# Softmax sums divided after the value product, and wo's norms and last weights placed elsewhere

## The chip, the cores and the metric

The kernel runs on one core of a Trainium2 chip. Its engines are TensorE (PE in the profile, with its weight loads as PEld), VectorE (DVE), ScalarE (ACT), GpSimd (POOL) and SyncE (SP, which here only issues DMAs). Each engine works through its own list of instructions in order. The metric is the device time of one execution in microseconds; the number before the change is the median of three runs.

## The reference, cut to what matters

One decoder layer on 1024 tokens of width 1024, in float32. Two SwiGLU half-steps stand around a token mixer with two branches, and the change touches branch A's softmax and the norms behind the mixer's output projection:

```
# branch A, for each head: scores against the selected keys, softmax, values
p = jax.nn.softmax(s, axis=-1)
o = p @ values
# the mixer's end, and the start of the second SwiGLU
y = (sigmoid(g_a) * (o_a @ w_up_a) + sigmoid(g_b) * (o_b @ w_up_b)) @ w_o
x = x + gt2 * rms_norm(y, g_post_mix)
h = rms_norm(x, g_pre_ffn2) * (1 + sc3) + sh3
x = x + 0.5 * gt3 * rms_norm(swiglu(h, w_gate2, w_up2, w_down2), g_post_ffn2)
```

## The kernel before

**Order.** The program is written in one order and then laid out for each engine by a scheduler ahead of time, with modelled costs; on the chip every engine keeps the order that it was given, and semaphores make it wait. Float32 products are made from three matmuls (`mm3`, lines L104 to L106), on a high part and a low part of each operand. `split` (L76, L77) makes these parts: ScalarE casts, VectorE subtracts; `psplit` (L81, L82) subtracts on GpSimd instead.

**Branch A** (`branch_a`) has four head pairs p, two heads e, four token groups g and two token tiles t = 2g, 2g + 1 in each. `scores` makes the masked scores of one tile in a buffer `aP` (six of them, shared in a ring) and their maximum (L1058, VectorE), takes the exponential on ScalarE with the row sum into `st` (L1061), inverts the sum on VectorE (L1062) and multiplies the whole tile by it on GpSimd (L1063). `mix` transposes the tile on TensorE (L1081, `apt`), splits it, and after the second tile of a group multiplies with the values (L1091, `apv`) into one PSUM bank of 512 columns, of which 256 are used. That bank, tag `o`, exists once. ScalarE copies one half out (L1095), VectorE adds the other (L1097); then the bank is free. There are 32 such products. During the third head pair, `combine_b` joins branch B's groups, eight times: small VectorE operations of 4 or 12 columns on `cM`, `ce` and `br` (L951 to L960) and three GpSimd operations (L962 to L964).

**wo.** The output projection is done in four quarters: token half h (0, 1), column half c (0, 1). A quarter has 96 matmuls: four token tiles j, eight pieces k of the contraction, three each. Its weights are 16 tiles (a high and a low part for each k) from pool `W`, which has 13; the next weights, of the second SwiGLU, use the same 13. With 13, the last three of a quarter must wait for the first three, so all four token tiles are worked on side by side in four PSUM banks, and end together. `evac` (L365, L366) takes a bank out and collects the row's squares. After each half, per token tile: `residual` adds up the squares, takes a reciprocal root and adds onto the residual stream `xt` (L1160), a DMA writes it away, and `prenorm` squares it on ScalarE (L1165), takes a second root and scales (L1168). A root is `rsqrt`, eight instructions of one column each (L88, L89, then three pairs of L94 and L95), on VectorE for four of the sixteen and on GpSimd for the other twelve. `xt` of half 1 is read, 2 MB at once, into a buffer of tag `z`; that of half 0 has tag `gab`.

**After wo.** `first_half` transposes half 0 (L208), scales it (L214, L216) and splits it into V[0] and V[1]; `second_half` does so with half 1 and makes V[2] to V[6] from sums and differences (L232). `gate_up` multiplies V[i] with weights for blocks b; the program has it start with V[0] and V[1] for three blocks (144 matmuls) and then go on to V[2].

Of the kernel before, what the change touches and what calls it, by code (L numbers as in the profile page):

```python
# [10 lines left out]
F32 = mybir.dt.float32  # L11
F32R = mybir.dt.float32r
# [8 lines left out]
D = 1024  # L21
# [18 lines left out]
class Layer:  # L40
# [453 lines left out]
        nc.vector.tensor_tensor(out1, out1, t[0], op=ALU.subtract)  # L494
        nc.vector.tensor_tensor(out2, out2, t[1], op=ALU.add)

    def load_w(self, W, src, n, name, rows=1024, per=None, split=None, rawp=None):

        nc = self.nc
        per = per or 1024 // n  # L500
        his, los = [], []
        nk = rows // P
        for k0 in range(0, nk, per):
            m = min(per, nk - k0)
            r = (rawp or self.rawp).tile([P, m, n], F32, name=f"{name}r", tag="raw")
            nc.sync.dma_start(r, src[k0 * P:(k0 + m) * P, :].rearrange("(k p) f -> p k f", p=P))
            for j in range(m):
                hi = W.tile([P, n], F32R, name=f"{name}h", tag="w")
                lo = W.tile([P, n], F32R, name=f"{name}l", tag="w")
                (split or self.split)(hi, lo, r[:, j, :])  # L510
                his.append(hi)
                los.append(lo)
        return his, los
# [457 lines left out]
    def branch_a(self, aw, ap, late, G, mask, off):  # L971
# [73 lines left out]
        def scores(p, e, g, t):  # L1045

            K, Q, n = KE[p % 2][e], QQ[:, e], (t + 1) * P
            Pm = ap.tile([P, S], F32, name="aP", bufs=NAP)[:, :n]
            mx = late.tile([P, 2], F32, name="mx", bufs=4)
            st = late.tile([P, 2], F32, name="st", bufs=4)  # L1050
            nb = (n + 511) // 512
            for c in range(nb):
                m = min(512, n - 512 * c)
                b = self.bank("as", tag=next(banks))
                self.mm3(b[:, :m], Q[:, 0, t, :], Q[:, 1, t, :],
                         K[:, 0, 512 * c:512 * c + m], K[:, 1, 512 * c:512 * c + m], True, True)
                mk = self.tri[:, 256 - n:] if t < 2 else mask[:, off[t] + 512 * c:off[t] + 512 * c + m]
                nc.vector.tensor_tensor_reduce(Pm[:, 512 * c:512 * c + m], b[:, :m], mk, -scale,  # L1058
                                               mx[:, 0:1] if c else 3.0e38,
                                               op0=ALU.add, op1=ALU.min, accum_out=mx[:, c:c + 1])  # L1060
            nc.scalar.activation(Pm, Pm, AF.Exp, bias=mx[:, nb - 1:nb], scale=-1.0, accum_out=st[:, 1:2])  # L1061
            nc.vector.reciprocal(st[:, 1:2], st[:, 1:2])  # L1062
            nc.gpsimd.tensor_tensor(Pm, Pm, st[:, 1:2].to_broadcast([P, n]), op=ALU.mult)  # L1063
            state[p, e, t] = Pm

        def mix(p, e, g, t):

            nj = 2 * g + 2
            if t == 2 * g:
# [18 lines left out]
            for j in range(nj):  # L1088
                q0 = max(0, j - 2 * g) * P
                for l in range(2):  # L1090
                    nc.tensor.matmul(b[:, q0:256], VV[p][:, j, e, :], pt[j // 4][l][:, j % 4, q0:],  # L1091
                                     start=j == 0 and l == 0, stop=j == nj - 1 and l == 1)
            main, oth = slice(64 * e, 64 * e + 64), slice(64 - 64 * e, 128 - 64 * e)
            tmp = late.tile([P, 256], F32, name="otmp", bufs=2)
            nc.scalar.copy(tmp[main, :], b[oth, :256])  # L1095
            od = of[g // 2][main, (g % 2) * 256:(g % 2 + 1) * 256]
            nc.vector.tensor_add(od, b[main, :256], tmp[main, :])  # L1097
            if p == 2:
                self.combine_b(late, state["oB"], 4 * e + g)
            if e == 1 and g == 0:  # L1100
# [72 lines left out]
def layer_kernel(ctx, tc, aps, out):  # L1173
# [136 lines left out]
    with pool("w3", 13) as W, pool("r5", 3) as L.rawp, pool("o2") as op:  # L1310
# [5 lines left out]
        with pool("zp") as zp:  # L1316
# [6 lines left out]
            ss = sums()  # L1323
            for h in range(2):
                ys[h] = L.big.tile([P, 4, D], F32, name=f"wy{h}", tag="big")
                xt = zp.tile([P, 4, D], F32, name=f"xt{h}", **(dict(tag="z", bufs=3) if h else dict(tag="gab")))
                nc.sync.dma_start(xt, L.x1[4 * h * P:(4 * h + 4) * P, :].rearrange("(t p) d -> p t d", p=P))
                for c in range(2):
                    cl = slice(c * 512, (c + 1) * 512)
                    wh, wl = L.load_w(W, aps["w_o"][0][:, cl], 512, "wo")  # L1330
                    for j in range(4):
                        b = L.bank("wo", tag="pj")
                        for k in range(8):
                            L.mm3(b, z[h][0][:, k, tok(j)], z[h][1][:, k, tok(j)], wh[k], wl[k], k == 0, k == 7)
                        L.evac(jk, b, ys[h][:, j, cl], G[:, cl], ss[4 * h + j][:, c:c + 1])
                for j in range(4):
                    t = 4 * h + j
                    L.residual(ys[h][:, j, :], xt[:, j, :], ss[t], ss[t][:, 2:3], nc.vector if t in (4, 6) else nc.gpsimd)
                    nc.sync.dma_start(x2[tok(t), :], xt[:, j, :])
                    L.prenorm(ys[h][:, j, :], xt[:, j, :], None, ss[t][:, 2:3], ss[t][:, 3:4], nc.vector if t in (5, 7) else nc.gpsimd)  # L1340
                if h == 0:
                    V[0], V[1] = bigv(0), bigv(1)
                    L.first_half(V, ys[0], range(8), sh, a3)
# [64 lines left out]
```

## Time and profile before

| | |
|---|---|
| median of 3 runs | 2521.93 us (2517.61 to 2523.97) |
| the profiled execution | 2520.3 us, of which the traced span is 2518.4 us |
| PE, DVE, ACT, POOL busy | 2357.4, 1611.1, 1094.7, 951.2 us |
| branch A | about 1463 to 1648 us after the span's start |
| wo's first three quarters | about 1711 to 1785 us, the end of the third among half 0's norms |
| wo's last quarter | 1795 to 1817 us |
| half 1's norms and V[2] | 1817 to 1886 us |

Times in the rows count from the start of the span. A busy PE is not a PE at its best: matmuls overlap, so the distance from one start to the next tells more than the duration shown.

### The profile page before, as it was taken

Reading aid. Unit: us, or ns where it says so; the run is one execution under the profiler, and the core shown is the slowest. Engines: PE = TensorE matmul, PEld = TensorE weight load, DVE = VectorE, ACT = ScalarE, POOL = GpSimd, SP = SyncE. Lnnn points to the kernel's source line nnn. Section 1 sums busy time; section 2 is a strip of 40 time slices with the busy share of each in tenths; the row PEclk is TensorE's granted clock in tenths of the full one; section 3 lists DMA queues with packets and bytes.
Section 4 is the critical chain, followed back from the end, with each engine's and each line's share of the span. In section 5 each row is a group of like instructions: output and inputs, shape, how many; then the busy total and the mean of one; then the engine's idle time right before and its main releaser. Section 6 shows DMA issues by size and latency. Waiting matters only on the chain.

```text
span 2518.4 us, 33990 instructions
## 1 busy us (share of the span) xinstructions
PE 2357.4 (94%) x11279; PEld 1978.4 (79%) x11279; DVE 1611.1 (64%) x3193; ACT 1094.7 (43%) x2342; POOL 951.2 (38%) x1109
## 2 busy tenths in 40 slices
PE   5799999999998999999989799899879999999997
PEld 4578887778787877889989677678658888888886
DVE  7866778754885145999963388874486554553455
ACT  5422322333454355777445466623443333333443
POOL 5675555400004433432243144601587454430012
PEclk9899999999998999999999799999989999999999
DMA  9234455761634233512421422154234323253134
GB/s 279 89 107 134 145 159 153 240 230 51 190 117 122 73 99 97 193 33 66 142 59 51 104 64 70 45 198 158 96 113 130 97 76 92 80 195 107 53 107 151
DMA packets 229804, 300.04 MB, mean 119 GB/s; under 512 B 23607, under 2 KB 144343, under 8 KB 229629
## 3 DMA queue, kind: packets, MB, share of 16 engines
q1 hardware_dynamic: 228988, 296.80, 37.4%
q8 instruction: 90, 1.47, 0.2%
q10 hardware_dynamic: 640, 1.07, 0.1%
q14 instruction: 86, 0.70, 0.1%
HBM read 233.98 MB, written 63.83 MB: 118 GB/s over the span
## 4 chain that ended last, share of the span: by engine, by line
PE 75%; DVE 11%; DMA 5%; issue 3%; ACT 3%; POOL 3%; SPq 0%; DVEq 0%; ACTq 0%; POOLq 0%
PE gu L104 9%; PE gu L105 9%; PE gu L106 9%; PE dn L105 6%; PE dn L106 6%; PE dn L104 6%; PE gpj L104 2%; PE gpj L105 2%; PE gpj L106 2%; PE bq L104 2%; DMA wr<-in_w_mod_dram 2%; PE bq L105 2%; PE bq L106 1%; PE apv L1091 1%; PE bv L104 1%
## 5 line engine op out<-in xcount | busy, mean ns | idle before, releaser
L104 PE MATMUL gu<-V,wh 128*128 128x512 f32 x1232 | 488.5, 397 | 18.9 <-ACT wh L76 9.3
L105 PE MATMUL gu<-V,wl 128*128 128x512 f32 x1232 | 487.3, 396 | 6.0 <-DVE wl L77 5.7
L106 PE MATMUL gu<-V,wh 128*128 128x512 f32 x1232 | 482.3, 394 | 4.5 <-DVE V L77 4.5
L77 DVE TENSOR_TENSOR wl<-rw,wh 128x512 fp32r<-128x512 f32 x232 | 214.1, 925 | 134.6 <-PE gu L105 93.7
L104 PEld LDWEIGHTS gu<-V,wh 128*128 128x128 f32 x1232 | 234.6, 191 | 73.3 <-ACT wh L76 11.3
L105 PEld LDWEIGHTS gu<-V,wl 128*128 128x128 f32 x1232 | 234.3, 190 | 59.7 <-DVE wl L77 8.9
L106 PEld LDWEIGHTS gu<-V,wh 128*128 128x128 f32 x1232 | 233.3, 190 | 56.5 <-DVE V L77 7.0
L105 PE MATMUL dn<-dh,al 128*128 128x512 f32 x704 | 275.6, 391 | 1.6 <-DVE al L77 1.6
L106 PE MATMUL dn<-dl,ah 128*128 128x512 f32 x704 | 274.4, 391 | 0.0
L104 PE MATMUL dn<-dh,ah 128*128 128x512 f32 x704 | 253.7, 391 | 6.0 <-DVE junk L197 6.0
L76 ACT CAST wh<-rw 128x512 fp32r<-128x512 f32 x232 | 140.1, 618 | 210.0 <-PE gu L106 126.3
L351 POOL TENSOR_TENSOR p<-p 128x512 f32<-128x512 f32 x86 | 129.9, 1511 | 247.3 <-DVE p L343 70.1
L343 DVE TENSOR_TENSOR p<-gu,p 128x512 f32<-128x512 f32 x252 | 170.0, 681 | 67.2 <-PE gu L106 35.6
L76 ACT CAST ah<-act 128x512 fp32r<-128x512 f32 x176 | 107.4, 621 | 182.3 <-PE dn L105 131.2
L77 DVE TENSOR_TENSOR al<-act,ah 128x512 fp32r<-128x512 f32 x176 | 118.0, 689 | 80.5 <-PE dn L105 42.5
L104 PEld LDWEIGHTS dn<-dh,ah 128*128 128x128 f32 x704 | 132.5, 188 | 33.9 <-DVE junk L197 6.4
L105 PEld LDWEIGHTS dn<-dh,al 128*128 128x128 f32 x704 | 132.7, 189 | 30.5 <-DVE al L77 3.2
L77 DVE TENSOR_TENSOR dl<-rd,dh 128x512 fp32r<-128x512 f32 x132 | 91.2, 692 | 101.4 <-PE dn L105 52.4
L106 PEld LDWEIGHTS dn<-dl,ah 128*128 128x128 f32 x704 | 132.9, 189 | 27.7
L349 ACT ACTIVATE p<-p 128x512 f32<-128x512 f32 x86 | 54.4, 633 | 215.4 <-DVE p L343 163.8
L185 DVE SCALAR_TENSOR_TENSOR macc<-wr,scol,macc 128x512 f32<-128x512 f32 x98 | 91.9, 938 | 56.0 <-DMA wr<-in_w_mod_dram 55.4
L76 ACT CAST dh<-rd 128x512 fp32r<-128x512 f32 x132 | 81.6, 618 | 83.3 <-PE dn L105 70.8
(465 smaller groups left out, 5465.4 us busy)
## 6 DMA issues: line engine op xcount, KB each, us to landing
rd<-in_w_down_dram SPq DMA_DIRECT2D x66, 512.0 KB
wr<-in_w_mod_dram SPq DMA_DIRECT2D x112, 256.0 KB
rw<-in_w_gate_dram SPq DMA_DIRECT2D x44, 512.0 KB
rw<-in_w_up_dram SPq DMA_DIRECT2D x44, 512.0 KB
act<-act SPq DMA_DIRECT2D x88, 256.0 KB
act<-p SPq DMA_DIRECT2D x86, 256.0 KB
wm<-in_w_mod_dram SPq DMA_DIRECT2D x32, 256.0 KB
x<-xt SPq DMA_DIRECT2D x16, 512.0 KB
```

The lines of the kernel that those rows point to most:

```text
L76: self.nc.scalar.copy(hi, src)
L77: self.nc.vector.tensor_sub(lo, src, f(hi))
L104: mm(out, ah, bh, start=start, stop=False)
L105: mm(out, al, bh, start=False, stop=False)
L106: mm(out, ah, bl, start=False, stop=stop)
L185: nc.vector.scalar_tensor_tensor(acc, r, self.scol[:, k:k + 1], acc, op0=ALU.mult, op1=ALU.add)
L343: nc.vector.tensor_tensor(x[m], bk, y[m], op=ALU.add)
L349: nc.scalar.activation(x[0], x[0], AF.Silu)
L351: nc.gpsimd.tensor_tensor(x[1], x[1], x[0], op=ALU.mult)
L1091: nc.tensor.matmul(b[:, q0:256], VV[p][:, j, e, :], pt[j // 4][l][:, j % 4, q0:], start=j == 0 and l == 0, stop=j == nj - 1 and l == 1)
```

## The change

Branch A no longer multiplies the exponentials by the inverse sums. The two sums of a token group go into the two columns of one `st` tile; after the product with the values, one VectorE instruction inverts both, TensorE transposes each column, spread over 128 columns, into the unused 256 columns of the product's bank, and VectorE multiplies the result by them (64 partitions by 256). All roots of wo's norms are on VectorE. The high parts of the last quarter's weights get a room of their own in tag `z`, and `xt` of half 1 has tag `gab` like that of half 0.

```diff
@@ load_w @@
-                hi = W.tile([P, n], F32R, name=f"{name}h", tag="w")
+                hi = W.tile([P, n], F32R, name=f"{name}h", tag="w") if room is None else room[:, k0 + j]
@@ branch_a, scores @@
-            st = late.tile([P, 2], F32, name="st", bufs=4)
+            if t == 2 * g:
+                state["st"] = late.tile([P, 2], F32, name="st", bufs=4)
...
-            nc.scalar.activation(Pm, Pm, AF.Exp, bias=mx[:, nb - 1:nb], scale=-1.0, accum_out=st[:, 1:2])
-            nc.vector.reciprocal(st[:, 1:2], st[:, 1:2])
-            nc.gpsimd.tensor_tensor(Pm, Pm, st[:, 1:2].to_broadcast([P, n]), op=ALU.mult)
+            nc.scalar.activation(Pm, Pm, AF.Exp, bias=mx[:, nb - 1:nb], scale=-1.0,
+                                 accum_out=state["st"][:, t % 2:t % 2 + 1])
@@ branch_a, mix @@
+            st = state["st"]
+            nc.vector.reciprocal(st, st)
+            for x in range(2):
+                nc.tensor.transpose(b[:, 256 + x * P:256 + (x + 1) * P], st[:, x:x + 1].to_broadcast([P, P]), self.ident)
             tmp = late.tile([P, 256], F32, name="otmp", bufs=2)
             nc.scalar.copy(tmp[main, :], b[oth, :256])
             od = of[g // 2][main, (g % 2) * 256:(g % 2 + 1) * 256]
             nc.vector.tensor_add(od, b[main, :256], tmp[main, :])
+            nc.vector.tensor_mul(od, od, b[main, 256:512])
@@ layer_kernel, wo @@
-                xt = zp.tile([P, 4, D], F32, name=f"xt{h}", **(dict(tag="z", bufs=3) if h else dict(tag="gab")))
+                xt = zp.tile([P, 4, D], F32, name=f"xt{h}", tag="gab")
...
-                    wh, wl = L.load_w(W, aps["w_o"][0][:, cl], 512, "wo")
+                    room = zp.tile([P, 8, 512], F32R, name="wohi", tag="z", bufs=3) if h and c else None
+                    wh, wl = L.load_w(W, aps["w_o"][0][:, cl], 512, "wo", hi=room)
...
-                    L.residual(ys[h][:, j, :], xt[:, j, :], ss[t], ss[t][:, 2:3], nc.vector if t in (4, 6) else nc.gpsimd)
+                    L.residual(ys[h][:, j, :], xt[:, j, :], ss[t], ss[t][:, 2:3], nc.vector)
                     nc.sync.dma_start(x2[tok(t), :], xt[:, j, :])
-                    L.prenorm(ys[h][:, j, :], xt[:, j, :], None, ss[t][:, 2:3], ss[t][:, 3:4], nc.vector if t in (5, 7) else nc.gpsimd)
+                    L.prenorm(ys[h][:, j, :], xt[:, j, :], None, ss[t][:, 2:3], ss[t][:, 3:4], nc.vector)
```

In the rows of order that follow, lines of the changed kernel from branch A on have higher numbers: L1097 has become L1102, L1160 L1166 and L1168 L1174.

The first place is VectorE's list in branch A's third head pair, where a product's result leaves its bank. Before, the add is the last reader of the bank:

```order
L1062 RECIPROCAL st<-st 128x1
L958 TENSOR_TENSOR cM<-cM,br 128x4
L1062 RECIPROCAL st<-st 128x1
L959 RECIPROCAL cM<-cM 128x4
L956 TENSOR_TENSOR br<-br,ce 128x3x4
L960 TENSOR_TENSOR ce<-ce,cM 128x12
L1097 TENSOR_TENSOR of<-apv,otmp 64x256
```

In the changed kernel the multiply (L1103) reads it too, and other work stands between the two:

```order
L1102 TENSOR_TENSOR of<-apv,otmp 64x256
L1059 ISA aP,mx<-as,mask 128x384
L1059 ISA mx 128x1
L77 TENSOR_TENSOR pt<-apt,pt 128x4x128
L1059 ISA aP,mx<-as,mask,mx 128x256
L1059 ISA mx 128x1
L957 TENSOR_TENSOR cM<-br 128x4
L1103 TENSOR_TENSOR of<-of,apv 64x256
```

The bank's last reader has moved back by up to six instructions; over the 32 products the number between L1102 and L1103 goes from none (nine times) to six (twice).

The second place is VectorE's list at the end of wo's last quarter (`wo` is its banks, `wy` the result of half 1). Before, the four evacuations stand close together, ahead of the first residual:

```order
L77 TENSOR_TENSOR wol<-wor,woh 128x512 x2
L77 TENSOR_TENSOR wl_17559<-re_17556,wh_17558 128x512
L77 TENSOR_TENSOR wl_17565<-re_17562,wh_17564 128x512
L366 TENSOR_TENSOR wy_17021<-wo,G_16537 128x512
L1158 TENSOR_TENSOR sums<-sums 128x1
L88 TENSOR_SCALAR rs_v<-sums 128x1
L89 TENSOR_SCALAR rs_y<-rs_v 128x1
L366 TENSOR_TENSOR wy_17021<-wo,G_16537 128x512
```

In the changed kernel, from the first evacuation of that quarter on, a whole norm stands between one evacuation and the next:

```order
L366 TENSOR_TENSOR wy_16989<-wo,G_16505 128x512
L1164 TENSOR_TENSOR sums<-sums 128x1
L88 TENSOR_SCALAR rs_v<-sums 128x1
L89 TENSOR_SCALAR rs_y<-rs_v 128x1
L94 TENSOR_SCALAR rs_t<-rs_y,rs_v 128x1
L95 TENSOR_SCALAR rs_y<-rs_t,rs_y 128x1
...
L95 TENSOR_SCALAR sums<-rs_t,rs_y 128x1
L1166 SCALAR_TENSOR_TENSOR xt_16990<-wy_16989,sums,xt_16990 128x1024
L366 TENSOR_TENSOR wy_16989<-wo,G_16505 128x512
```

Half 1's norms have moved in among the quarter's evacuations, and the two weight splits that stood ahead of them come after the third one. TensorE's list there has 24 matmuls for one token tile after the other, in place of four tiles side by side.

The third place is SyncE's list of DMAs (`xt` read from `x` is the residual stream of half 1, `x` written from `xt` the result, `re` the second SwiGLU's first weights). Before, `xt` is read ahead of half 0's writes:

```order
L506 DMA wor<-in_w_o_dram 128x2x512 x7
L1327 DMA xt_17022<-x_77 128x4x1024
L506 DMA wor<-in_w_o_dram 128x2x512
L1339 DMA x_16057<-xt_16549 128x1024 x4
L506 DMA wor<-in_w_o_dram 128x2x512 x2
```

In the changed kernel it comes after them and after four weight loads:

```order
L1346 DMA x_16025<-xt_16517 128x1024 x4
L506 DMA wor<-in_w_o_dram 128x2x512 x2
L271 DMA re_17505<-in_w_gate_dram 128x4x128
L271 DMA re_17511<-in_w_up_dram 128x4x128
L271 DMA re_17517<-in_w_gate_dram 128x4x128
L271 DMA re_17523<-in_w_up_dram 128x4x128
L1333 DMA xt_16990<-x_77 128x4x1024
L271 DMA re_17529<-in_w_gate_dram 128x4x128
L1346 DMA x_16025<-xt_16990 128x1024 x2
L271 DMA re_17535<-in_w_up_dram 128x4x128
```

The read of `xt` has moved behind half 0's writes and four of the twelve `re` loads, and the writes of half 1's first two tiles have moved ahead of the sixth.

## Rows read from the trace of the kernel before

**Rows 1.** The page: the chain that ended last, by engine.

```profile
PE 75%; DVE 11%; DMA 5%; issue 3%; ACT 3%; POOL 3%; SPq 0%; DVEq 0%; ACTq 0%; POOLq 0%
```

**Rows 2.** Stretch: PE, PEld, DVE, ACT, POOL busy (count), PE clock, DMA share, GB/s.

```profile
1463.00:1540.00 77.00, 72.02 (x464) 62.27 (x462) 66.26 (x202) 56.32 (x139) 38.78 (x36) 0.98 0.23 64
1540.00:1615.00 75.00, 59.64 (x362) 50.19 (x361) 67.66 (x202) 46.64 (x117) 43.82 (x39) 0.93 0.22 63
...
1817.00:1850.00 33.00, 28.79 (x128) 22.64 (x127) 23.63 (x56) 18.21 (x36) 25.17 (x42) 1.00 0.62 203
1850.00:1890.00 40.00, 28.34 (x99) 19.73 (x97) 34.47 (x34) 16.79 (x29) 36.09 (x22) 0.75 0.14 41
```

**Rows 3.** VectorE's groups, 1540 to 1615: count, busy us, mean ns, idle before.

```profile
L1097 DVE TENSOR_TENSOR of<-apv,otmp 64x256 f32<-64x256 f32 x12 | 5.1, 421 | 0.2
L952 DVE TENSOR_TENSOR cM<-cM,br 128x4 f32<-128x4 f32 x6 | 4.9, 823 | 0.0
L957 DVE TENSOR_TENSOR cM<-br 128x4 f32<-128x4 f32 x6 | 4.3, 711 | 0.1
L958 DVE TENSOR_TENSOR cM<-cM,br 128x4 f32<-128x4 f32 x6 | 4.0, 662 | 0.0
...
L1062 DVE RECIPROCAL st<-st 128x1 f32<-128x1 f32 x23 | 3.5, 153 | 0.3 <-ACT aP L1061 0.2
L956 DVE TENSOR_TENSOR br<-br,ce 128x12 f32<-128x12 f32 x6 | 3.5, 578 | 0.0
...
L954 DVE TENSOR_TENSOR ce<-br,cM 128x12 f32<-128x12 f32 x6 | 0.9, 155 | 0.0
```

**Rows 4.** Busy by stretch, as in rows 2: instructions on branch A's score tiles alone.

```profile
1540.00:1615.00 75.00, 20.47 (x112) 13.94 (x112) 20.26 (x36) 20.64 (x48) 28.38 (x24) 0.93 0.22 63
```

**Rows 5.** TensorE in order of time: three transposes and the next start.

```profile
1547.27 0.49 PE L1081 MATMUL apt<-ident,aP 128*128 128x128 f32 x3
1547.52 0.48 PE L104 MATMUL as<-KK,aq 128*128 128x512 f32 x1
```

**Rows 6.** Waits in branch A: us in total, times, longest.

```profile
DVE aP L1058 <- PE apt L1081: 8.4, 15, 1.6
...
PE apv L1091 <- DVE of L1097: 3.9, 4, 1.5
```

**Rows 7.** GpSimd in order of time: first and last instruction of half 0's norms.

```profile
1754.96 0.19 POOL L1158 TENSOR_TENSOR sums<-sums 128x1 f32<-128x1 f32 x1 [118.72 <-ACT junk L365]
...
1783.73 0.26 POOL L95 TENSOR_SCALAR sums<-rs_t,rs_y 128x1 f32<-128x1 f32 x1
```

**Rows 8.** VectorE's groups, 1809 to 1850.

```profile
L1160 DVE SCALAR_TENSOR_TENSOR xt<-wy,sums,xt 128x1024 f32<-128x1024 f32 x4 | 6.1, 1536 | 1.8 <-POOL sums L95 1.8
...
L94 DVE TENSOR_SCALAR rs_t<-rs_y,rs_v 128x1 f32<-128x1 f32 x12 | 3.1, 268 | 0.0
L1168 DVE TENSOR_SCALAR wy<-xt,sums 128x1024 f32<-128x1024 f32 x4 | 3.0, 754 | 3.3 <-POOL sums L95 3.3
L366 DVE TENSOR_TENSOR wy<-wo,G 128x512 f32<-128x512 f32 x4 | 2.8, 689 | 2.9 <-ACT junk L365 2.9
...
L95 DVE TENSOR_SCALAR rs_y<-rs_t,rs_y 128x1 f32<-128x1 f32 x8 | 1.6, 206 | 0.1
```

**Rows 9.** TensorE: wo's last matmul, gate_up's first, and the last stall.

```profile
1816.49 0.39 PE L106 MATMUL wo<-wol,z 128*128 128x512 f32 x1
1816.72 0.39 PE L104 MATMUL gu<-V,wh 128*128 128x512 f32 x1
...
1886.28 0.50 PE L106 MATMUL gu<-V,wh 128*128 128x512 f32 x1 [0.95 <-DVE V L77]
```

**Rows 10.** VectorE: the first instruction of second_half.

```profile
1848.58 1.28 DVE L232 TENSOR_TENSOR wy<-wy,wy 128x512 f32<-128x512 f32 x1 [1.51 <-ACT wy L216]
```

**Rows 11.** Busy by stretch while xt of half 1 was read.

```profile
1758.00:1764.00 6.00, 6.00 (x29) 4.95 (x28) 1.44 (x2) 1.15 (x2) 5.23 (x17) 1.00 1.02 410
```

**Rows 12.** SyncE in order of time: the third re load.

```profile
1810.82 0.37 SPq L271 DMA_DIRECT2D re<-in_w_gate_dram  x1
```

More of the change, by code (lines that the diff above doesn't have):

```diff
@@ L495, in rope, with load_w @@
         nc.vector.tensor_tensor(out2, out2, t[1], op=ALU.add)
-    def load_w(self, W, src, n, name, rows=1024, per=None, split=None, rawp=None):
+    def load_w(self, W, src, n, name, rows=1024, per=None, split=None, rawp=None, hi=None):
         nc = self.nc
-        per = per or 1024 // n
+        per, room = per or 1024 // n, hi
         his, los = [], []
```

## The prediction

> **What bounds the kernel now.** I read the chain that ended last first: 75% of it is TensorE and 11% VectorE [rows 1], so time is won where TensorE stands still or waits for VectorE. The table by stretch shows where. From 1463 to 1540 us, the first half of branch A, TensorE is busy for 72.0 of 77 us: it is the bound. From 1540 to 1615 us, the third head pair, it is VectorE with 67.7 of 75 us, and TensorE has 59.6. Behind wo, from 1850 to 1890 us, TensorE is busy for 28.3 of 40 us at a granted clock of 0.75, while VectorE has 34.5 and GpSimd 36.1: there TensorE waits for V [rows 2].
>
> **Branch A: the third head pair.** GpSimd loses its 64 multiplies; no GpSimd time is on the path here, but something else hangs on it. VectorE's smallest operations, 4 or 12 columns, take 823, 711, 662 and 578 ns where one of the same kind takes 155 [rows 3]. The excess is 6 x (0.67 + 0.56 + 0.51 + 0.42) = 12.9 us. They have two inputs in SBUF, and GpSimd is at work for 43.8 of the 75 us, 28.4 of them on score tiles [rows 2, 4]; so I take them to be held up by GpSimd, and 28.4/43.8 of the excess, 8.4 us, to go. VectorE also loses 23 reciprocals, 3.5 us, and gains 12 times a reciprocal (0.15) and a multiply out of PSUM of the shape of L1097 (0.42), 6.9 us [rows 3]. 67.7 - 8.4 - 3.5 + 6.9 = 62.7; with the 7.3 us that it stands idle now, the stretch takes 70.0: **-5.0 us**. Bounds: 0, if VectorE's relief is not on the path, and -8.4.
>
> **Branch A: TensorE.** 32 products get two transposes each. Three of that shape take 0.25 us from start to start [rows 5], so two take some 0.2 us with the change of operand. In the third pair TensorE has room (59.6 + 2.4 of 70), for the other 20 products it is the bound: 20 x 0.2 = **+4.0 us**.
>
> **Branch A: the bank.** The product's only bank now also waits for the multiply and for what stands ahead of it in VectorE's list, up to six instructions. Queued behind are the next product's matmuls, and behind these all of TensorE's list. TensorE has waited for this bank four times, 3.9 us together [rows 6]. Bounds: 0, if other matmuls fill the time, and 32 x 1.1 = 35 us, if every product waits for a multiply (0.42) and some 0.7 us of work between. The trace is nearer to the lower end (4 waits in 32); I take the four waits a microsecond longer: **+4 us**.
>
> **Branch A: the ring of score tiles.** VectorE waits 8.4 us in all for a free `aP` [rows 6]. Without the GpSimd pass a tile's life is shorter. Between 0 and -8.4, and mostly where TensorE is the bound anyway: **-2 us**. The four together: +1.
>
> **wo, half 0.** GpSimd works from 1754.96 to 1783.99 us on these eight roots [rows 7], and the transposes wait for the last. On VectorE a root is three pairs of 0.268 + 0.206 and two more of about 0.2: 1.83 us; eight roots and four sums 15.4, four residuals 6.1, four scalings 3.0 [rows 8], and four weight splits that stand ahead of the last scaling, 2.8: 27.3 us against 29.0. **-2 us**. Bounds: -5, if roots that are interleaved overlap, and +1.
>
> [...] The rows have 0.27 and 0.21 for the dependent pairs, so the sum stands on these.
>
> **wo, half 1: the largest term.** With room for all its weights the last quarter can do one token tile after the other, as its order now has it. A matmul starts every 0.23 us [rows 9], 24 make a tile: the tiles end 16.5, 11, 5.5 and 0 us before the quarter's end, where now all four end together. Per tile VectorE has an evacuation 0.69, a sum 0.2, two roots 3.66, a residual 1.54 and a scaling 0.75 [rows 8]: 6.85 us, four of them 27.4. Six weight splits and two sums of gate_up lie between, 8 x 0.69 = 5.5. So VectorE starts second_half some 32.9 us after the first tile's end, 16.4 us behind the quarter's end. Now it starts at 1848.58, 31.9 us behind gate_up's first matmul at 1816.72 [rows 9, 10]. That is 15.5 us earlier, and TensorE, with the same 144 matmuls to bridge the gap, waits that much less for V; its last stall there ends at 1886.28 us [rows 9]. There is enough to win: between 1817 and 1890 us it starts 227 instructions in 73 us [rows 2]; 195 at 0.23 and 32 transposes at 0.1 would take 48. From the 15.5 I take off 2.5 for waits that the new order of DMAs brings: the sixth `re` load stands behind the writes of two residuals, and ScalarE's cast of it ahead of the third evacuation. **-13 us**. What hides the weights: they are needed 5.5 us apart once gate_up begins. `xt`, 2 MB at the 410 GB/s seen [rows 11], takes 5.1 us and has the quarter's first 5.5 us, if it is issued by its start. Bounds: -20, if the interleaved roots overlap by half, and 0, if `xt` is late (below).
>
> **The sum.** +1 - 2 - 13 = -14: the profiled execution's 2520.3 us becomes 2506.3. The median of the runs is 1.6 above that execution, so I say 2508 us.
>
> **The rivals.** (a) *The bank is the new bound, and the kernel gets slower.* For it speaks that the bank is single and that the list puts up to six instructions ahead of its release; against it, that only four waits show now [rows 6]. At 1.1 us for each of 32 products it costs 35 instead of 4: 2539 us. It decides from 32 x 0.8 us on, which eats the -18 that is left without it and 7.6 more. [...] Chance 0.13. (b) *`xt` of half 1 comes too late.* It stands behind four `re` loads, and the third of these was issued only at 1810.82, near the quarter's end [rows 12], because the weight tiles were taken; then all four norms follow the quarter as now, the term of 13 is gone, and it is 2521 us, no change. Against it: the quarter now takes 8 of the 13 tiles and leaves 5, enough for the first two loads' parts, which frees their buffers. Chance 0.15. (c) *The small operations' relief is off the path*: +5, about 2513 us. The 7.3 us idle of VectorE speak for it, the 90% against. Chance 0.2. (d) *More*: the ring and the overlapped roots give their best, 2497 us. Chance 0.12. The forecast itself, 2501 to 2513 us: 0.4.
>
> **How the numbers follow.** This measurement tells about 0.3%, 7.6 us, from no change: 2514.3 to 2529.5 is "same". Faster: 0.4 + 0.12, and 0.14 of (c): 0.66. Same: (b) less 0.02, 0.06 of (c) and 0.01 of (a): 0.20. Slower: 0.14. The range goes from (d) to (b): 2496 to 2522 us, with (a)'s upper part left out.
>
> **What would show it.** Right: `cM` rows near 155 ns in branch A; L366 of half 1's tiles 5 to 6 us apart; second_half's first L232 some 16 us behind the last `wo` matmul; a granted clock near 1.0 where 0.75 stands now. Wrong: TensorE waiting for the new multiply tens of times; VectorE's first residual of half 1 waiting for a DMA. The forecast fails if VectorE, which takes all that GpSimd loses, is late at every product.

## The result and the profile after

The changed kernel takes 2503.56 us in the median of four runs (2498.26 to 2506.22), against 2519.77 us for four of the kernel before; the ratio is 0.9931, with a 95% interval of 0.9916 to 0.9946. That is 16 us or 0.7% faster, and the prediction said 2508. The single profiled execution is 22 us shorter than that of before (a span of 2496.1 us after 2518.4), and 5.4 us of this are no effect of the change. Up to branch A every engine has the same list of instructions in both programs, yet its first score matmul starts at 1446.27 us before and at 1440.83 us after; over the fourteen profiled executions of this study it starts anywhere from 1440.3 to 1449.6. So times are compared below by the length of stretches, each from one landmark of the program to the next. Where the order is the same these repeat closely: branch A's whole stretch takes 199.3 to 199.7 us in the four executions with the order of before, and 191.0 to 193.3 in the four with that of after.

The landmarks, all of TensorE, are the first score matmul of branch A (`as`), the last of its 320 value matmuls (`apv`), the first `wo` matmul, the 289th (the last quarter's first), the last, and the last `gate_up` matmul. Each length is a difference of two starts in the trace.

| stretch, us | before | after | difference | foreseen |
|---|---|---|---|---|
| branch A, to its first `apv` | 25.6 | 18.7 | -6.9 | |
| branch A, to its last `apv` (with the row above) | 199.4 | 191.4 | -8.0 | +1 |
| last `apv` to first `wo` | 65.2 | 69.0 | +3.8 | 0 |
| first `wo` to the last quarter | 84.0 | 81.0 | -3.0 | -2 |
| the last quarter | 21.7 | 21.7 | 0 | 0 |
| last `wo` to the last `gate_up` | 448.9 | 439.1 | -9.8 | -13 |
| sum | | | -17.0 | -14 |

The chain that ended last, by engine, answers to [rows 1]: TensorE has less of it, VectorE more.

```profile
PE 72%; DVE 13%; DMA 7%; ACT 3%; issue 3%; POOL 2%; SPq 0%; DVEq 0%; ACTq 0%; POOLq 0%
```

The table by stretch of the changed kernel, with the columns of [rows 2]; the first two stretches lie 13 us earlier than there and the others 12 (the last is 2 us longer). Around the third head pair GpSimd has lost half of its work; VectorE has lost under 4 us, and TensorE has gained 6. Behind wo, the 4.2 us that TensorE had been idle from 1817 to 1850 are gone. In the last row it still stands still for 12 of 42 us.

```profile
1450.00:1527.00 77.00, 75.22 (x521) 66.53 (x519) 69.06 (x214) 58.96 (x146) 5.73 (x6) 1.00 0.26 73
1527.00:1602.00 75.00, 65.76 (x411) 54.73 (x411) 63.97 (x215) 48.79 (x124) 20.92 (x20) 0.95 0.22 63
1805.00:1838.00 33.00, 33.00 (x158) 27.34 (x157) 27.14 (x51) 19.99 (x34) 16.37 (x12) 1.00 0.53 167
1838.00:1880.00 42.00, 30.00 (x118) 21.92 (x117) 37.76 (x35) 14.26 (x26) 36.60 (x24) 0.88 0.25 74
```

**Where branch A gains.** In the kernel before, three engines in order of time show how the stretch begins: start, duration, instruction, and in brackets the idle time before it. The first score tile is ready to be multiplied at 1458.45, GpSimd takes 1.68 us, and the transposes of that tile start at 1462.31. TensorE does not stand still for that pass, since its list has other matmuls ahead of the transposes. What it waits for before its first product, but for 0.24 us, is VectorE, three times (0.70, 1.11 and 1.82 us). VectorE is in operations of `combine_b` there: two of its eight calls lie here and not in the third head pair. Beside GpSimd's passes of 1458.45 and 1461.12 two of these operations take 1.65 and 1.68 us and end within 0.02 us of the pass; in the changed kernel, where GpSimd is idle, they take 0.16. From 1467 to 1470, behind the longest wait, the granted clock is 0.52.

```profile
1446.27 0.64 PE L104 MATMUL as<-KK,aq 128*128 128x512 f32 x1
...
1458.45 1.68 POOL L1063 TENSOR_TENSOR aP<-aP,st 128x896 f32<-128x896 f32 x1 [36.06 <-DVE st L1062]
1458.50 1.65 DVE L951 TENSOR_TENSOR cM<-br 128x4 f32<-128x4 f32 x1
...
1460.47 0.50 PE L104 MATMUL as<-KK,aq 128*128 128x512 f32 x1 [0.70 <-DVE mx L1058]
...
1461.12 1.90 POOL L1063 TENSOR_TENSOR aP<-aP,st 128x1024 f32<-128x1024 f32 x1 [0.99 <-DVE st L1062]
...
1461.35 1.68 DVE L952 TENSOR_TENSOR cM<-cM,br 128x4 f32<-128x4 f32 x1
...
1462.31 0.38 PE L1081 MATMUL apt<-ident,aP 128*128 128x128 f32 x2
...
1466.92 0.39 PE L104 MATMUL vpj<-wv,gbuf 128*128 128x256 f32 x1 [1.82 <-DVE aV L77]
...
1471.91 0.39 PE L1091 MATMUL apv<-pt,aV 128*128 128x256 f32 x1 [0.24 <-ACT pt L76]
```

After, there is no such pass and no place for it in TensorE's list, and TensorE has no wait of 0.15 us or more up to its first product: the transposes come 10.9 us behind the first score matmul in place of 16.0, and the first product 18.7 us in place of 25.6.

```profile
1440.83 0.60 PE L104 MATMUL as<-KK,aq 128*128 128x512 f32 x1
...
1451.70 0.55 PE L1082 MATMUL apt<-ident,aP 128*128 128x128 f32 x3
...
1459.49 0.75 PE L1092 MATMUL apv<-pt,aV 128*128 128x256 f32 x3
```

From there on the two kernels keep that distance within 1.1 us: at the 80th, 160th and 240th `apv` the changed one is ahead by 5.8, 7.3 and 6.6 us.

**The third head pair.** VectorE's groups of the changed kernel, 1527 to 1602, answer to [rows 3] (count, busy us, mean ns, idle before). The four that were long have indeed become short, 148 to 300 ns after 578 to 823. But the reciprocals, and above all the multiplies, take 7 us, as the prediction had it.

```profile
L1102 DVE TENSOR_TENSOR of<-apv,otmp 64x256 f32<-64x256 f32 x13 | 5.5, 421 | 0.6 <-ACT otmp L1100 0.3
L1103 DVE TENSOR_TENSOR of<-of,apv 64x256 f32<-64x256 f32 x12 | 5.0, 418 | 0.3
...
L1096 DVE RECIPROCAL st<-st 128x2 f32<-128x2 f32 x13 | 2.0, 152 | 0.4 <-ACT aP L1062 0.4
...
L956 DVE TENSOR_TENSOR br<-br,ce 128x12 f32<-128x12 f32 x6 | 1.8, 300 | 0.0
...
L957 DVE TENSOR_TENSOR cM<-br 128x4 f32<-128x4 f32 x6 | 1.7, 284 | 0.0
...
L958 DVE TENSOR_TENSOR cM<-cM,br 128x4 f32<-128x4 f32 x6 | 1.3, 212 | 0.0
...
L952 DVE TENSOR_TENSOR cM<-cM,br 128x4 f32<-128x4 f32 x6 | 0.9, 148 | 0.0
```

**The bank.** TensorE's waits in branch A answer to [rows 6]: 3.2 us in five waits for the multiply, where it was 3.9 in four for the add, and one more of 2.0 us, which the list puts down to `cM`.

```profile
PE apv L1092 <- DVE of L1103: 3.2, 5, 1.0
...
PE apv L1092 <- DVE cM L952: 2.0, 1, 2.0
```

VectorE in order of time shows what that last one is. The add (L1102) is done at 1572.02, and without the multiply the bank would be free then. Behind it stands `combine_b`'s first operation, which waits 1.81 us for a DMA, and only behind that the multiply, which frees the bank at 1574.32. TensorE's next product starts at 1574.47. So the danger of rival (a), a bank held by what stands ahead of its last reader, is real, and it struck once.

```profile
1571.62 0.40 DVE L1102 TENSOR_TENSOR of<-apv,otmp 64x256 f32<-64x256 f32 x1
1573.83 0.16 DVE L951 TENSOR_TENSOR cM<-br 128x4 f32<-128x4 f32 x1 [1.81 <-DMA br<-bd]
1573.91 0.41 DVE L1103 TENSOR_TENSOR of<-of,apv 64x256 f32<-64x256 f32 x1
```

**Between branch A and wo.** Half of the 8 us goes again. The rows stand in order of time (SyncE's queue, VectorE, TensorE) and are read from the last one up. On TensorE, `upa` waits 3.13 us for VectorE's `gab`, and VectorE has waited for a DMA. On SyncE's queue, the loads of `gab` stand behind the second load of `wubr`, which waits for a free buffer until 1635.49, 9 us behind the load ahead of it. In the list of the kernel before, four `gab` loads stand ahead of this `wubr`.

```profile
1626.40 0.97 SPq L506 DMA_DIRECT2D wuar<-in_w_up_a_dram  x2
...
1635.49 0.37 SPq L506 DMA_DIRECT2D wubr<-in_w_up_b_dram  x1
1635.96 0.41 SPq L1139 DMA_DIRECT2D gab<-gd  x1
...
1640.59 1.28 DVE L1150 SCALAR_TENSOR_TENSOR gab<-gab,upa 128x512 f32<-128x512 f32 x2 [2.11 <-DMA gab<-gd]
...
1641.33 0.50 PE L104 MATMUL upa<-oA,wup 128*128 128x512 f32 x1 [3.13 <-DVE gab L1150]
```

**Half 1's norms.** `xt` of half 1 was issued at 1774.63, ahead of the quarter, and the evacuations of the quarter's four tiles (L366) come 5.5, 5.4 and 7.0 us apart. second_half's first instruction (L232) starts at 1823.08, 19.1 us behind the last `wo` matmul at 1804.0; in [rows 9, 10] it was 32.1 us.

```profile
1774.63 0.37 SPq L1333 DMA_DIRECT2D xt<-x  x1
...
1788.78 0.69 DVE L366 TENSOR_TENSOR wy<-wo,G 128x512 f32<-128x512 f32 x1 [3.44 <-ACT junk L365]
...
1794.28 0.69 DVE L366 TENSOR_TENSOR wy<-wo,G 128x512 f32<-128x512 f32 x1 [1.37 <-ACT junk L365]
...
1799.72 0.69 DVE L366 TENSOR_TENSOR wy<-wo,G 128x512 f32<-128x512 f32 x1 [0.36 <-ACT junk L365]
...
1806.70 0.68 DVE L366 TENSOR_TENSOR wy<-wo,G 128x512 f32<-128x512 f32 x1
...
1823.08 0.69 DVE L232 TENSOR_TENSOR wy<-wy,wy 128x512 f32<-128x512 f32 x1 [1.20 <-ACT wy L216]
```

**What waits next.** The last of these rows is TensorE's largest stall in the last stretch of the table. Followed back from it, the rows lead from a weight's cast on ScalarE to GpSimd's L288, one of the sums and differences of weights that `gate_up` makes. V is not what is late there.

```profile
1843.34 1.71 POOL L288 TENSOR_TENSOR rw<-s,rw 128x512 f32<-128x512 f32 x1
...
1845.08 1.14 ACT L76 CAST wh<-rw 128x512 fp32r<-128x512 f32 x2 [1.52 <-POOL rw L288]
...
1845.75 1.31 PE L104 MATMUL gu<-V,wh 128*128 128x512 f32 x2 [5.24 <-ACT wh L76]
```

GpSimd is busy for 10.00 of 10 us from 1835 to 1845 and from 1845 to 1855, and the granted clock goes from 1.00 between 1820 and 1835 to 0.94 in the first of these stretches and 0.55 in the second, behind the 5.24 us in which TensorE had nothing to do.

### The profile page after: what moved, and what is told of

Same layout as the page of the kernel before. It is cut to its first block, busy times and chain, and to the rows that moved or that the text cites. A ratio compares the mean times of both kernels' runs of the same rounds, so it can differ in the third digit from the quotient of the medians.

```text
span 2496.1 us, 33927 instructions
## 1 busy us (share of the span) xinstructions
PE 2348.3 (94%) x11343; PEld 1974.1 (79%) x11343; DVE 1619.6 (65%) x3295; ACT 1092.6 (44%) x2342; POOL 834.2 (33%) x943
## 4 chain that ended last, share of the span: by engine, by line
PE 72%; DVE 13%; DMA 7%; ACT 3%; issue 3%; POOL 2%; SPq 0%; DVEq 0%; ACTq 0%; POOLq 0%
PE gu L104 8%; PE gu L105 8%; PE gu L106 8%; PE dn L105 6%; PE dn L106 6%; PE dn L104 6%; DMA wr<-in_w_mod_dram 3%; PE gpj L104 2%; PE gpj L105 2%; PE gpj L106 2%; PE bq L104 2%; DVE macc L185 2%; PE bq L105 1%; PE bq L106 1%; DVE wl L77 1%
## 5 line engine op out<-in xcount | busy, mean ns | idle before, releaser
L77 DVE TENSOR_TENSOR wl<-rw,wh 128x512 fp32r<-128x512 f32 x232 | 219.2, 948 | 131.3 <-PE gu L105 93.3
```

Of the source, the lines that this page charges most:

```text
L77: self.nc.vector.tensor_sub(lo, src, f(hi))
```

## The experiments

All stretches are those of the table above. Where an expectation says 191.7 us for branch A, the two transposes of the last sums are counted with it.

**The two halves of the change apart.** One kernel has only branch A's part of the diff, one only wo's, and of wo's part one has only the roots and one only the room:

```diff
a_only:      branch A's lines of the diff; wo as before
wo_only:     wo's lines of the diff; branch A as before
norms_only:  before, and
-  L.residual(..., nc.vector if t in (4, 6) else nc.gpsimd)
+  L.residual(..., nc.vector)          (prenorm alike)
room_only:   before, and
+  room = zp.tile([P, 8, 512], F32R, name="wohi", tag="z", bufs=3) if h and c else None
+  wh, wl = L.load_w(W, aps["w_o"][0][:, cl], 512, "wo", hi=room)      (xt of half 1: tag "gab")
```

> Only branch A divides at its end; wo is as before. Theory from the two traces: TensorE wins 8.0 us inside branch A and gives 3.8 us back between branch A and wo, so about -4 us against before (2516 where before is 2520). Rival, the sum of the prediction on record: +1 us, no change (2521). Under a second rival, that the bank binds, it would be slower than before.

> Only wo is changed (all roots on VectorE, room for the last quarter's weights, xt of half 1 in the other tag); branch A is as before. Theory from the traces: -2.9 us up to wo's last matmul and -9.8 us behind it, together about -12.7 us (2507 where before is 2520). The prediction on record has -15 us (2505). Rival: the two parts are not additive, since what branch A wins is lost in a wait that wo has anyway; then this alone gives the full -16 us.

> Only the twelve roots go from GpSimd to VectorE; no room, so the last quarter's four token tiles still end together. Theory: the norms of half 0 win 3 us, those of half 1 all follow the quarter's end and cost VectorE 27 us there, so 0 to -4 us (2516 to 2520). Rival: the roots are most of the gain, about -10 us (2510).

> Only the room for the last quarter's high parts (and xt of half 1 in the other tag); the roots stay where they were, twelve on GpSimd. Theory: the token tiles end one after the other and three norms are done before the quarter ends, so most of the -9.8 us behind wo remains: -6 to -10 us (2510 to 2514). Rival: roots of some 0.26 us a step on GpSimd, with the transfers between engines, fill the time between two tiles, and the room alone is worth under 3 us (2517 or more).

| | median, us | ratio to before (95%) | branch A | to wo | to last quarter | wo's end to gate_up's |
|---|---|---|---|---|---|---|
| before | 2519.64 | | 199.4 | 65.2 | 84.0 | 448.9 |
| a_only | 2514.63 | 0.9977 (0.9965 to 0.9989) | 193.3 | 67.3 | 83.9 | 448.3 |
| wo_only | 2504.73 | 0.9936 (0.9923 to 0.9949) | 199.7 | 65.2 | 80.7 | 438.9 |
| norms_only | 2508.92 | 0.9957 (0.9945 to 0.9969) | 199.5 | 65.2 | 76.9 | 445.8 |
| room_only | 2510.20 | 0.9964 (0.9951 to 0.9977) | 199.3 | 65.2 | 84.1 | 439.2 |

By the medians branch A's part is worth 5 us and wo's 15; by the stretches, the last quarter included (22.7 us in a_only, 21.6 or 21.7 in the others), 3.7 and 13.1, which add up to 16.8 of the full change's 17.0. Each acts where the landmarks of the full change said. The expectation for the roots alone fell: they win 10.7 us, not 0 to 4, and its rival was right. Half 0 becomes 7.1 us shorter with them, and only 3.0 with the room as well. Part of it shows in TensorE's waits ahead of half 0's transposes: 0.34 and 1.82 us with the roots alone,

```profile
1775.27 0.44 PE L208 MATMUL tr<-ident,wy 128*128 128x128 f32 x2 [0.34 <-DVE wy L1168]
1777.53 0.44 PE L208 MATMUL tr<-ident,wy 128*128 128x128 f32 x2 [1.82 <-DVE wy L1168]
```

and 3.79 and 1.71 in the changed kernel:

```profile
1772.26 0.69 PE L208 MATMUL tr<-ident,wy 128*128 128x128 f32 x2 [3.79 <-DVE wy L1174]
1774.65 0.69 PE L208 MATMUL tr<-ident,wy 128*128 128x128 f32 x2 [1.71 <-DVE wy L1174]
```

The room does what it was taken to do, -9.7 us behind wo, even with the roots on GpSimd; with the roots on VectorE as well it is -10.0, so they add almost nothing there. The theory to test next for half 0: with room, the scheduler can split the last quarter's weights early, and puts these splits among half 0's norms.

**Branch A: which tiles, and what the division costs.** Three kernels change the changed kernel's branch A:

```diff
@@ first_head_old (COND is p == 0 and e == 0) and pair2_old (p == 2); in mix, no division where COND holds @@
+            if COND:
+                s1 = state["st"][:, t % 2:t % 2 + 1]
+                nc.vector.reciprocal(s1, s1)
+                nc.gpsimd.tensor_tensor(Pm, Pm, s1.to_broadcast([P, n]), op=ALU.mult)
@@ pair2_dummy @@
+            if p == 2:
+                dm = late.tile([P, S], BF, name="dm", bufs=1)
+                nc.gpsimd.tensor_tensor(dm[:, :n], Pm, mx[:, 0:1].to_broadcast([P, n]), op=ALU.mult)
```

The fourth, no_divide, leaves out the reciprocals (L1096), the transposes of the sums (L1098) and the multiply (L1103), so branch A's values stay undivided.

> The changed kernel, but the first of the eight heads (8 of 64 score tiles) is divided before the product as in the kernel before, on GpSimd; the other seven heads divide at the end. Measured on branch A's stretch from its first score matmul to its last product, 199.4 us before and 191.7 after. Theory: most of the gain is won while the pipeline fills, since the first transposes no longer wait for a GpSimd pass; then these 8 tiles alone bring back most of it, 197 to 200 us. Rival: the gain comes from VectorE's relief in the third head pair; then it stays at 191 to 193 us.

> The changed kernel, but the third head pair (16 of 64 score tiles) is divided before the product on GpSimd; the others divide at the end. Theory of the prediction: VectorE's small operations are held up by GpSimd again, the rows of cM and ce take 26 us in all instead of 10, and the stretch grows by about 5 us (197). Rival: the small operations lengthen but are off the path, and with 8 fewer pairs of transposes the stretch stays within 1 us (191 to 192).

> The changed kernel, with one more GpSimd multiply per score tile of the third head pair that reads the same tile, is as long, and writes a tile that nobody reads; nothing on the path waits for its result. Theory: the mere presence of GpSimd slows VectorE's small operations (0.5 to 0.8 us each as before, where they take 0.15 to 0.3 now). Rival: they were slow because they waited for results of GpSimd or for their place; then they stay at 0.15 to 0.3 us. The time of the stretch tells what it is worth: 191 to 193 us if this is off the path, 195 to 197 if it is on it.

> The changed kernel without the division: no reciprocals, no transposes of the sums, no multiply, so branch A's values stay undivided. It measures what dividing at the end costs. The prediction on record has 4.0 us for the transposes and 4 us for the bank: the stretch falls by 8 us, to 184. Theory from the trace: 32 pairs of transposes at 0.21 us are 6.8 us, of which the part in the first, second and fourth head pair counts, and the bank costs about 1: 186 to 187 us. Rival: VectorE's 32 multiplies and 32 reciprocals, 18 us, are on the path, and the stretch falls below 180.

| start of the n-th `apv` behind the first score matmul, us | 1st | 80th | 160th | 240th | 320th | median of runs, ratio (95%) |
|---|---|---|---|---|---|---|
| before | 25.6 | 67.2 | 114.1 | 160.6 | 199.4 | 2518.81 |
| after | 18.7 | 61.4 | 106.8 | 154.0 | 191.4 | |
| first_head_old | 26.7 | 68.4 | 113.7 | 158.8 | 196.0 | 2506.34, 0.9952 (0.9932 to 0.9972) |
| pair2_old | 18.9 | 61.6 | 111.7 | 149.1 | 190.6 | 2502.46, 0.9936 (0.9921 to 0.9952) |
| pair2_dummy | 18.7 | 61.4 | 111.2 | 157.9 | 195.8 | 2503.98, 0.9946 (0.9929 to 0.9962) |
| no_divide | 18.7 | 61.8 | 104.4 | 141.2 | 176.0 | 2479.95, 0.9853 (0.9838 to 0.9868) |

A head pair has 80 of these matmuls, so the columns close one pair after the other. With 8 of 64 tiles divided as before, the first product is 8.0 us later again, and at the end 4.6 us are left of that (196.0, a microsecond short of the 197 expected): more than half of the gain is that of the pipeline's filling. The run does not tell in which way the passes cost it. They are a stage that the first tiles go through, and they lengthen VectorE's two `combine_b` there, which take 1.64 and 1.68 us again in the same two operations; TensorE's three longest waits before its first product (0.94, 0.83 and 2.20 us) are for VectorE. With the third pair divided as before, the stretch is 0.8 us *shorter*: what VectorE is relieved of there and what it and TensorE are given cancel.

The relief itself is on the path, as pair2_dummy shows. Nothing waits for GpSimd's extra pass, and six groups of the small operations take 260 to 546 ns:

```profile
L954 DVE TENSOR_TENSOR ce<-br,cM 128x12 f32<-128x12 f32 x6 | 3.3, 546 | 0.0
L957 DVE TENSOR_TENSOR cM<-br 128x4 f32<-128x4 f32 x6 | 3.1, 525 | 0.0
...
L952 DVE TENSOR_TENSOR cM<-cM,br 128x4 f32<-128x4 f32 x6 | 1.6, 260 | 0.0
```

TensorE's order is that of the changed kernel for the first 706 instructions of branch A. For 99 us these start within 0.1 us of those of the changed kernel; by 108 us they are over 4 us late, and the stretch ends 4.4 us later. In between TensorE waits 1.25, 0.40 and 2.66 us for VectorE, where the changed kernel has 0.26 and 0.75. One of the small operations that hold VectorE up starts at 1540.33, in GpSimd's pass of 1539.75 to 1541.64, and ends at 1541.67:

```profile
1539.75 1.89 POOL L1066 TENSOR_TENSOR dm<-aP,mx 128x1024 bf16<-128x1024 f32 x1 [2.32 <-ACT aP L1062]
1540.33 1.34 DVE L954 TENSOR_TENSOR ce<-br,cM 128x12 f32<-128x12 f32 x1
...
1550.79 0.62 PE L104 MATMUL as<-KK,aq 128*128 128x512 f32 x1 [2.66 <-DVE mx L1059]
```

So GpSimd's presence slows them, and here the stretch pays 4.4 us for it. In these rows the operation lasts for the rest of GpSimd's pass and ends 0.03 us behind it, as the two long ones in the kernel before end 0.02 and 0.01 us behind theirs.

no_divide shows what dividing at the end costs: 15.4 us, twice the 8 that the prediction had for transposes and bank. The first pair costs nothing (61.4 and 61.8), the second 2.8, the third 10.4 (from 106.8 to 154.0 in place of 104.4 to 141.2) and the fourth 2.6. In the third pair TensorE stands idle for 6.6 us at a granted clock of 0.93, and without the division for 1.1 at 1.00; so more than half of it is waiting, in the pair where VectorE has most to do. Over the whole stretch TensorE is idle for 15.6 us in place of 7.8 and busy for 175.9 in place of 168.2, so TensorE's own work, the 64 transposes among it, is half of the cost. The scheduler laid TensorE's list out anew from 27 us on, so the shares of the pairs are those of two orders, and no price of one product.

**Three edits on the changed kernel, and all together.** The first tests the theory on half 0, the second one on `gab` (its place in SyncE's list is the wait), the third makes less work of the division:

```diff
wo_psplit:
-   wh, wl = L.load_w(W, aps["w_o"][0][:, cl], 512, "wo", hi=room)
+   wh, wl = L.load_w(W, aps["w_o"][0][:, cl], 512, "wo", hi=room, split=L.psplit if h and c else None)
gab_pool:
+   E = nc.gpsimd if m < 2 else nc.sync
-   nc.sync.dma_start(ga, self.gd[m])
+   E.dma_start(ga, self.gd[m])                 (gb alike)
pair_divide: (st is 128x8x2 for a head pair; nothing is divided behind a single product)
+   if e == 1 and g % 2 == 0:
+       st, c = state["st", p], self.bank("apr", tag="tr")
+       nc.vector.reciprocal(st[:, 2 * g:2 * g + 4], st[:, 2 * g:2 * g + 4])
+       wide = late.tile([P, 4, 2, 64], F32, name="wide", bufs=1)
+       nc.scalar.copy(wide, st[:, 2 * g:2 * g + 4].to_broadcast([P, 4, 2, 64]))
+       for x in range(4):
+           nc.tensor.transpose(c[:, x * P:(x + 1) * P], wide[:, x].rearrange("p e m -> p (e m)"), self.ident)
+       nc.vector.tensor_mul(of[g // 2], of[g // 2], c)
```

> The changed kernel, with the low parts of the last quarter's weights made on GpSimd instead of VectorE (eight subtractions); nothing else moves. Measured from wo's first matmul to the start of its last quarter: 84.0 us before, 81.1 after, 76.9 with the norms on VectorE and no room. Theory: the room lets the scheduler put the quarter's eight weight splits (0.69 us each, 5.5 us) among half 0's norms on VectorE, which is why the change wins only 3 of 7 us there; then this gives 77 us, and the kernel 2499.5. Rival: GpSimd's subtractions of 1.3 us slow VectorE's norms, or give the weights late; then 81 us or more and 2503 or more.

> The changed kernel, with the first four loads of gab issued by GpSimd, which has nothing else to do there, instead of SyncE, where they stand behind the second load of wubr. Measured from branch A's last product to wo's first matmul: 65.2 us before, 68.9 after. Theory: the loads wait in SyncE's list for a free weight buffer, and that is the 3.1 us stall of upa; then 65.5 to 66 us, and the kernel 2500.5. Rival: the transfers are late of themselves, since the buffers of gab come free late or the queue is taken; then 68 to 69 us and no change.

> The changed kernel, with the division moved from each of 32 products to the end of each half of a head pair, for both heads at once: 8 reciprocals, 8 widening copies on ScalarE, 32 transposes and 8 multiplies of 128x512 in place of 32 reciprocals, 64 transposes and 32 multiplies of 64x256. The product's bank no longer waits for it. Branch A's stretch is 191.7 us after and 176.0 without any division. Theory: the 15.7 us are the work of the division on VectorE (18 us) and TensorE (7 us); 10 of these 25 us are left, so about 6 us of cost: 182 us, the kernel 2494. Rival: the chain at each pair's end, reciprocal, copy, transposes, multiply, split, about 2.5 us, is now waited for: 186 to 188 us.

> The three edits above together. Theory: they act in three places, so they add up: 4 + 3 + 9.5 us off the changed kernel, 2487 us. Rival: what branch A wins is lost again in the wait for the weights and gab behind it, whose loads start no earlier; then 2493 or more.

| | median, us | ratio to before (95%) | branch A | to wo | to last quarter | wo's end to gate_up's |
|---|---|---|---|---|---|---|
| before | 2517.12 | | 199.4 | 65.2 | 84.0 | 448.9 |
| after (other runs) | 2503.56 | 0.9931 (0.9916 to 0.9946) | 191.4 | 69.0 | 81.0 | 439.1 |
| wo_psplit | 2496.81 | 0.9918 (0.9902 to 0.9935) | 191.0 | 69.1 | 78.2 | 438.4 |
| gab_pool | 2499.45 | 0.9917 (0.9899 to 0.9935) | 191.6 | 66.5 | 80.3 | 438.6 |
| pair_divide | 2505.83 | 0.9953 (0.9935 to 0.9971) | 199.1 | 67.2 | 79.6 | 438.8 |
| all3 | 2504.41 | 0.9942 (0.9925 to 0.9959) | 199.9 | 66.2 | 77.6 | 437.9 |

wo_psplit takes 2.8 us out of half 0 (but 1.1 back in the last quarter, 22.8 for 21.7): the splits were most of what the room had cost there. gab_pool takes 2.5 of the 3.8 us back. GpSimd's queue issues the first `gab` load at 1638.71, 0.8 us behind the last product at 1637.89, where SyncE's had come 3.7 us behind it: the place in the list was most of the wait, and the other 1.3 us stay open.

```profile
1638.71 0.80 POOL L1140 DMA_DIRECT2D gab<-gd  x1 [26.03 <-PE apv L1098]
```

Each is worth some 2 us by its stretch. The intervals of these two overlap that of the changed kernel, so neither is shown to beat it by the runs, and the two were run together only with pair_divide. That one is a miss: 182 us were expected, 186 to 188 by its rival, and with a quarter of the multiplies and half of the transposes branch A is as long as before the change. all3 misses with it, 2504 us for 2487. TensorE's two largest waits in pair_divide's branch A, `apt` for VectorE's `pt` (6.6 us in nine) and `as` for `mx` (4.2 in ten), have 3.5 and 2.0 us in the changed kernel. The first is a wait for a bank of tag `tr`, of which the spread sums now take one of two. But the scheduler also laid branch A out anew, and TensorE is idle for 21.0 us of the stretch in place of 15.6, 5.4 of the 7.7 us; so the cause stays open.

## Why the prediction was right

The direction, the size (16 us for 14) and the place of the largest term held; the terms of branch A did not, and that the sum fits is in part luck.

- **wo, half 1** (-13): right in its mechanism, and somewhat too large. `xt` was not late, so rival (b) is out. VectorE came to second_half 19.1 us behind the quarter, for 16.4: the third evacuation was followed by a norm, two weight splits and a scaling of 1.79 us beside GpSimd (0.75 at 1798.61, where GpSimd is idle). The room alone wins 9.7 us, so this term stands on the order of the token tiles and hardly on the roots. Of the 13 us that second_half is earlier, 9.8 came through, since the weights from GpSimd are late next, which the prediction did not name. The "granted clock near 1.0" held until 1835; from 1845 to 1855 it was 0.55.
- **wo, half 0** (-2): -3.0, within its bounds, but as the sum of two larger numbers: -7.1 from the roots, and 4.1 back with the room, most of it (2.8, by wo_psplit) for weight splits that it brings forward. The roots alone come out near the bound "-5, if roots that are interleaved overlap", and beyond it.
- **Third head pair** (-5.0): this step failed. The small operations did shrink, but by the 240th `apv` against the 160th the pair takes 47.2 us after 46.5. The prediction took VectorE for the bound there and counted what it loses against what it gains, with the transposes as free. The relief is on the path (4.4 us in pair2_dummy), but dividing costs 10.4 us there (no_divide, an order of its own), where 6.9 had been counted for the stretch; in the sum pair2_old shows nothing won. Rival (c) had this number, and not the reason: it held the relief to be off the path.
- **Transposes and bank** (+4, +4): a pair of transposes takes 0.23 us where a transpose follows (20 of 22 places) and 0.15 before a score matmul, near the 0.2 that was taken. Waits for the bank grew from 3.9 to 5.2 us, so rival (a) did not come. In the one wait of 2.0 us the next product, in other columns of the bank, began at 1574.47, 0.15 us behind the end of the multiply. no_divide puts the division's whole cost at 15.4 us, for the 8 of these two terms and the 6.9 inside the -5.0: near in the sum, and not in the place.
- **Ring of score tiles** (-2): the largest miss of branch A is what this term left out. The prediction looked at waits for a free tile, and its rows begin at 1463 us, 17 us behind the branch's first score matmul. 6.9 us were won before the first product, in the filling, and first_head_old shows that the first head's passes had cost them. That they did so partly by holding up VectorE, the relief that the prediction had put in the third pair, is what the rows say; how much of it that is, no run separates.
- **Left out**: 3.8 us lost between branch A and wo, since the scheduler put the `gab` loads behind a load that waits for a buffer (gab_pool gives 2.5 of them back). The prediction looked for moved DMAs at wo alone.

Branch A with the way to wo came out at -8.0 + 3.8 = -4.2 for +1, and wo at -12.8 for -15. So a sum that fits to 3 us holds an error of 5 one way and of 2 the other, and the 5 is itself what is left of larger ones: 6.9 us won in the filling, nothing in the third pair for -5.0, and 3.8 lost behind it.

## What to carry to other kernels

Where a pass is taken out of a pipeline, price its start apart from its course: in the course the pass is hidden behind other tiles, and while it fills little else hides it. Ask as well whom the pass slows down: here small operations of VectorE that take 0.16 us without GpSimd took 1.65 and 1.68 beside its passes and ended within 0.02 us of them. When a buffer is added, ask what the scheduler will do earlier because of it, and on which engine: here the room gained 9.7 us at one place and cost 4 at another, most of it by weight splits that were free to move. Compare kernels of one scheduler by stretches between landmarks, which repeat here within 0.4 to 2.3 us, and not by whole spans, of which these start branch A 9 us apart with the same program ahead of it.

## What was not expected of the hardware

- Two roots interleaved on VectorE took hardly longer than one. In one root alone, the pair L94, L95 takes 0.56 us from start to start; two roots side by side take 0.61 for both their pairs. The prediction had this as a bound alone. VectorE in order of time, in the changed kernel:

```profile
1790.51 0.27 DVE L94 TENSOR_SCALAR rs_t<-rs_y,rs_v 128x1 f32<-128x1 f32 x1
...
1791.07 0.27 DVE L94 TENSOR_SCALAR rs_t<-rs_y,rs_v 128x1 f32<-128x1 f32 x1
...
1796.19 0.45 DVE L94 TENSOR_SCALAR rs_t<-rs_y,rs_v 128x1 f32<-128x1 f32 x2
...
1796.80 0.45 DVE L94 TENSOR_SCALAR rs_t<-rs_y,rs_v 128x1 f32<-128x1 f32 x2
```

  So in these rows nearly half of a lone chain's time (0.56 us a pair, for 0.30 with two chains) is time that another chain could use. The two whole roots from 1795.07 to 1797.50 take 1.2 us each, for the 1.83 of the prediction.
- Some large operations took longer as well where VectorE and GpSimd were both at work: VectorE's L232 takes 0.69 us at 1823.08, where GpSimd is idle, and 1.75 at 1850.10, where it is busy; GpSimd's own subtraction of 128x512 takes 1.28 us at 1839.20, where VectorE is idle, and 1.73 at 1841.65, where it is busy. In order of time:

```profile
1839.20 1.28 POOL L82 TENSOR_TENSOR V<-wy,V 128x512 fp32r<-128x512 f32 x1
...
1841.65 1.73 POOL L82 TENSOR_TENSOR V<-wy,V 128x512 fp32r<-128x512 f32 x1
...
1850.10 1.75 DVE L232 TENSOR_TENSOR wy<-wy,wy 128x512 f32<-128x512 f32 x1
```
